# A macaron block on one core: the up projections' fast products as wide matmuls on high and low parts side by side

## The chip, the cores and the metric

The kernel runs on one core of a Trainium2 chip. The metric is the device time of one execution in microseconds. Five engines work beside each other, each on its own queue of instructions in a fixed order: TensorE (PE, with its weight loads shown apart as PEld) multiplies matrices into eight banks of accumulation memory (PSUM); VectorE (DVE) and ScalarE (ACT) work on elements; GpSimd (POOL) and SyncE (SP) here mostly issue DMA transfers.

## The reference

Input x has 512 tokens of 1024 features, all in float32. The block is a feed-forward network with half weight (ffn1), a mixer of a short convolution and chunked gated linear attention, a second feed-forward network (ffn2) and a last norm.

```python
def swiglu(x, w_gu, w_down):
    g, u = jnp.split(x @ w_gu, 2, axis=-1)
    return (jax.nn.silu(g) * u) @ w_down
...
x = x + 0.5 * swiglu(rmsnorm(x, norm_ffn1_g), ffn1_w_gu, ffn1_w_down)   # 1024 -> 2 x 2816 -> 1024
x = x + hybrid_mixer(rmsnorm(x, norm_mix_g), ...)
x = x + 0.5 * swiglu(rmsnorm(x, norm_ffn2_g), ffn2_w_gu, ffn2_w_down)
return rmsnorm(x, final_norm_g)
```

The change is in `x @ w_gu` of both feed-forward networks, the up products.

## The kernel before, in words

**Precision.** A float32 product is made of three: every factor is split into a rounded high part and the remainder, its low part, and the kernel sums weight-high × input-high, weight-high × input-low and weight-low × input-high. A weight tile is cast by ScalarE to its high part (`wh`, L331) and VectorE subtracts to get the low part (`wl`, L332). Three buffers of each exist.

**Fast products.** Most of an up product is done in *sets*. A set takes 256 columns of g and 256 of u, 512 tokens in two halves of 256, and 1024 features in two halves, and computes its 2 × 2 × 2 block product with seven products in place of eight, named m1, p2, q6, p5, q7, p4, p3. Each has 512 features, 256 columns and 256 tokens. There are nine sets in each feed-forward network; the first columns are plain products (L366 and L380). The weights' side of the seven products is built in memory from four loaded blocks a11, a12, a21, a22, each 512 KB (128 × 1024 floats): S3 = a11 + a21 by VectorE (L318); then, by DMAs that accumulate into their target (L309, issued by GpSimd), a21 += a22, a11 += a21 and a12 += a11. m1 reads a11 before its add and q6 reads it after; p2 reads a12 before its add and p3 after; q7 reads S3. Ten slots hold these tiles, and a load (L291, issued by SyncE) into a slot waits until its last reader is done. So a11's slot can take a new load only once a12's add has read it, and of the tiles that S3 sums one is loaded into such a slot. The tokens' side (`Operands`) is built once per feed-forward network, during its first set.

**One product** (`Set.run`, L479 on) is 24 matmuls (L502) of 128 columns of weights against 256 tokens: three kinds of high and low, four feature tiles, two halves of columns `e`. The two halves share one bank of 512 floats. Products accumulate into shared banks named a, b, c: m1, q6, q7 and p4 add up in b, p2 in a, p5 and p3 in c. What must be kept on the way is copied out by ScalarE (L507, L510). In every set but the first, m1 is copied from bank b into bank a (L507, the *fork*), and p2 adds onto it, so that bank a ends as g of one token half. Six banks circulate.

**Order.** The Python program writes the instructions down in the order in which each engine gets them, save that a scheduler lets an instruction pass another where their inputs allow. `order()` (L76) lists the products; `Weights.issue` runs three products ahead of the matmuls, so casts, low parts and DMAs of a product stand in the queues that far ahead. `done()` (L722 on) hangs the work on results behind a product: the silu of g (L727, L740), u (L730), and the products of the two (L734, L476). In the second feed-forward network `natural()` transposes one of eight tiles of x after a set's p3 (L771) by TensorE, and ScalarE copies it back (L772).

Of the kernel before, what the change touches and what calls it, by code (L numbers as in the profile page):

```python
# [8 lines left out]
F32 = mybir.dt.float32  # L9
F32R = mybir.dt.float32r  # L10
# [83 lines left out]

PLAIN1, PLAIN2 = 4, 4
PLAN = []
STEPS = []
# [6 lines left out]
        PLAN.append(u)  # L106


def sets(mat, pairs):
# [70 lines left out]
def block_kernel(ctx: ExitStack, tc: tile.TileContext, xT, vecs, gf, gup, wgl, wts, out):  # L180
# [6 lines left out]
    ps = ctx.enter_context(tc.tile_pool(name="ps", bufs=6, space=bass.MemoryType.PSUM))  # L187
    pa = ctx.enter_context(tc.tile_pool(name="pa", bufs=2, space=bass.MemoryType.PSUM))

    cnt = [0]  # L190
# [11 lines left out]
    def tile_of(pool, shape, dtype=F32):  # L202
        cnt[0] += 1
        return pools[pool].tile(shape, dtype, tag=pool, name=f"{pool}{cnt[0]}")

    def T(dtype=F32):
        return tile_of("tp", [P, S], dtype)

    def MM():
        cnt[0] += 1  # L210
        return ps.tile([P, S], F32, tag="mm", name=f"mm{cnt[0]}")

    def AUX():
        cnt[0] += 1
# [24 lines left out]
    class Weights:  # L239
# [239 lines left out]
    class Set:  # L479
# [34 lines left out]
        def first(self):  # L514
# [4 lines left out]
            nc.vector.tensor_tensor(out=t, in0=self.bank["a"], in1=self.v["m1"], op=ALU.add)  # L519
            return t  # L520

    class Operands:

        ORDER = ("m1", "p2", "p5", "q6", "q7", "p4", "p3")

        def __init__(self, b):
            self.b = b
            self.parts = {}  # L530
            self.sums = set()

# [19 lines left out]
        def make(self, p):  # L552
            if p in self.parts:
                return
            i = self.ORDER.index(p)
            if i > 0:
                self.make(self.ORDER[i - 1])
            v = self.sum(p)
            h, l = (tile_of("op", [P, 1024], F32R) for _ in range(2))
            hv, lv = (t.rearrange("p (k t) -> p k t", t=HW) for t in (h, l))  # L560
            nc.scalar.copy(hv, v)
            nc.vector.tensor_tensor(out=lv, in0=v, in1=hv.bitcast(F32), op=ALU.subtract)
            self.parts[p] = (h, l)
# [86 lines left out]
    def ffn(up, down, norm, nxt, plain, at):  # L650
        xh, xl = norm.h, norm.l
        rows = []

        def finish(k):
            if k == at:
# [64 lines left out]
        def up_set(i):  # L720
            h = new_hid()

            def done(s, p):
                bank, v = s.bank, s.v
                if p == "p2":
                    s.g1 = T()
                    nc.scalar.activation(s.g1, s.first(), AF.Silu)  # L727
                if p == "q7":
                    u2 = T()
                    nc.vector.scalar_tensor_tensor(out=u2, in0=bank["c"], scalar=-1.0, in1=v["q7"],  # L730
                                                   op0=ALU.mult, op1=ALU.subtract)
                    s.u2 = u2
                if p == "p4":
                    nc.vector.scalar_tensor_tensor(  # L734
                        out=h[:, :, :HW], in0=pair(bank["b"]), scalar=-1.0, in1=pair(s.g1),
                        op0=ALU.mult, op1=ALU.mult)
                if p == "p3":
                    g2 = T()
                    nc.vector.tensor_tensor(out=g2, in0=bank["c"], in1=v["q6"], op=ALU.add)
                    nc.scalar.activation(g2, g2, AF.Silu)  # L740
                    mul(h[:, :, HW:], pair(s.u2), pair(g2))
                    if nxt is None and i < KD:
                        natural(i)
                    for w in range(WIDE):
                        if i == 4 * w + 4 - plain // 2:
                            downs.append(down_operands(w))
                            downs[w].early()

            return Set(xo, done)

        def pair(t):
            return t.rearrange("p (e t) -> p e t", t=HW)

        run_sets(up_set)

        def split_hid(k):

# [4 lines left out]
            return h, l  # L762

        down_product(full(down, KF), split_hid, downs, nxt)

    def natural(i):

# [736 lines left out]
    with phase("small2", f=1, tp=6, v=4, qk=2, g=1, y=4, small=1):  # L1504
        W.phase(4, 5)
        n2 = Norm(V_G2)
        mixer(nm, n2)
# [46 lines left out]
```

## Time and profile before

| | |
|---|---|
| median of 3 runs | 1181.64 us (1181.12 to 1182.07) |
| the profiled execution | 1180.99 us |
| its span, first to last instruction | 1179.3 us |
| granted TensorE clock, mean | 0.999 of full |
| up sets of ffn1, from the chain | 50.15 to 231.58 us |
| up sets of ffn2, from the chain | 878.47 to 1063.37 us |
| matmuls of 256 columns in sets (L502), all stages | 3584 + 1792 |

An entry such as "L332 DVE TENSOR_TENSOR wl<-f,wh" means line 332 of the program, run on VectorE, writing a `wl` tile from an `f` and a `wh` tile. In the groups of instructions the columns are total busy time, mean duration in ns, and the idle time of the engine just before, with what ended it. In the chain of waits a row is start, length, engine and line. In the windows the columns are TensorE busy, its weight loads, VectorE, ScalarE, GpSimd, then granted clock, DMA share and GB/s. A waits row names who waited for whom, the total, how often, and the longest.

### The profile page before, as it was taken

The page shows a single profiled execution, that of the slowest core. Times are in us where ns is not written, and L with a number is a line of the kernel's source. Part 1 is how long each engine was busy: PE and PEld are TensorE (multiplying, and loading weights), DVE is VectorE, ACT ScalarE, POOL GpSimd, SP SyncE. Part 2 cuts the span into 40 slices and gives each one's busy share as a digit, 9 for nine tenths or more (in the row PEclk, how much of TensorE's full clock was granted, in tenths as well). Part 3 has the DMA queues.
Part 4 walks back from the last instruction along what each step waited for, and adds up shares of the span by engine and source line. Part 5 has one row for each costly group of instructions (what it writes and reads, how often), then busy time and mean ns, then how long its engine had stood idle before and what let it go on. Part 6 is the DMA issues. An engine that isn't in the chain of part 4 may idle for free.

```text
span 1179.3 us, 19168 instructions
## 1 busy us (share of the span) xinstructions
PE 1170.9 (99%) x7794; PEld 1080.7 (92%) x7794; DVE 868.9 (74%) x1027; ACT 634.3 (54%) x790; POOL 117.4 (10%) x153
## 2 busy tenths in 40 slices
PE   9999999999999999999999999999999999999997
PEld 8899999988888889999999998998889999998886
DVE  7985656896568965767697787685598566579955
ACT  6564455674435655565565576544355554566543
POOL 0010101101010111100110100000001111001100
PEclk9999999999999999999999999999999999999999
DMA  9388777678524388777677766531638767757721
GB/s 350 79 210 197 171 193 178 158 199 206 212 85 113 87 207 223 189 180 200 180 196 192 199 199 186 141 109 44 232 68 211 181 180 175 190 153 186 178 83 72
DMA packets 62600, 200.25 MB, mean 170 GB/s; under 512 B 6864, under 2 KB 13136, under 8 KB 62512
## 3 DMA queue, kind: packets, MB, share of 16 engines
q0 software_dynamic: 18784, 68.17, 31.7%
q1 hardware_dynamic: 39088, 126.37, 30.9%
q10 hardware_dynamic: 4640, 4.49, 1.1%
q8 instruction: 61, 1.00, 0.3%
q14 instruction: 27, 0.22, 0.1%
HBM read 124.55 MB, written 8.39 MB: 113 GB/s over the span
## 4 chain that ended last, share of the span: by engine, by line
PE 97%; ACT 1%; issue 1%; DVE 1%; ACTq 0%; POOL 0%; POOLq 0%
PE mm L502 53%; PE mm L625 12%; PE mm L366 11%; PE mm L380 7%; PE mm L838 4%; PE aux L625 4%; PE aux L838 1%; PE aux L1161 1%; PE aux L1142 1%; PE aux L1120 1%; PE aux L1164 0%; PE aux L224 0%; PE aux L1121 0%; PE mm L857 0%; PE aux L771 0%
## 5 line engine op out<-in xcount | busy, mean ns | idle before, releaser
L331 ACT CAST wh<-f 128x1024 fp32r<-128x1024 f32 (+1 forms) x341 | 356.2, 1047 | 406.3 <-PE mm L502 207.4
L332 DVE TENSOR_TENSOR wl<-f,wh 128x1024 fp32r<-128x1024 f32 (+1 forms) x341 | 413.3, 1217 | 154.1 <-ACT wh L331 141.3
L502 PE MATMUL mm<-op,wh 128*128 128x256 f32 x3584 | 471.1, 284 | 0.4 <-ACT mm L507 0.4
L502 PEld LDWEIGHTS mm<-op,wh 128*128 128x128 f32 x3584 | 447.9, 192 | 2.2 <-ACT mm L507 0.8
L502 PE MATMUL mm<-op,wl 128*128 128x256 f32 x1792 | 251.5, 283 | 0.0
L502 PEld LDWEIGHTS mm<-op,wl 128*128 128x128 f32 x1792 | 231.2, 192 | 0.1
L309 POOL DMA_DIRECT2D f<-f x126 | 108.9, 869 | 929.0 <-DVE wl L332 542.2
L625 PE MATMUL mm<-wh,op 128*128 128x512 f32 x432 | 106.9, 389 | 0.0
L625 PEld LDWEIGHTS mm<-wh,op 128*128 128x128 f32 x432 | 80.9, 188 | 16.7
L366 PE MATMUL mm<-op,wh 128*128 128x512 f32 x384 | 91.0, 389 | 0.0
L366 PEld LDWEIGHTS mm<-op,wh 128*128 128x128 f32 x384 | 72.0, 188 | 14.9
L380 PE MATMUL mm<-op,wh 128*128 128x512 f32 x256 | 64.2, 393 | 0.0
L625 PE MATMUL mm<-wl,op 128*128 128x512 f32 x216 | 57.7, 389 | 0.0
L380 PEld LDWEIGHTS mm<-op,wh 128*128 128x128 f32 x256 | 48.1, 189 | 10.3
L318 DVE TENSOR_TENSOR f<-f,f 128x1024 f32<-128x1024 f32 x42 | 51.3, 1222 | 0.8
L625 PEld LDWEIGHTS mm<-wl,op 128*128 128x128 f32 x216 | 40.6, 188 | 8.4
L366 PE MATMUL mm<-op,wl 128*128 128x512 f32 x192 | 47.4, 389 | 0.0
L366 PEld LDWEIGHTS mm<-op,wl 128*128 128x128 f32 x192 | 36.0, 188 | 7.5
L510 ACT COPY tp<-mm 128x512 f32<-128x512 f32 x68 | 39.6, 583 | 0.0
L601 DVE TENSOR_TENSOR op<-hidw,op 128x1024 fp32r<-128x1024 f32 x28 | 34.0, 1219 | 1.1 <-ACT op L600 1.0
L380 PE MATMUL mm<-op,wl 128*128 128x512 f32 x128 | 34.3, 389 | 0.0
L416 ACT ACTIVATE op<-X,vec 128x512 fp32r<-128x512 f32 x23 | 16.5, 719 | 31.8 <-DVE X L859 24.3
(269 smaller groups left out, 1042.5 us busy)
## 6 DMA issues: line engine op xcount, KB each, us to landing
f<-wts SPq DMA_DIRECT2D x219, 512.0 KB, 4.5
f<-f POOLq DMA_DIRECT2D x126, 512.0 KB, 5.3
X<-xT SPq DMA_DIRECT2D x8, 256.0 KB, 5.3
xs<-X POOLq DMA_DIRECT2D x8, 256.0 KB, 2.3
ga<-tp ACTq DMA_DIRECT2D x8, 256.0 KB, 3.2
gb<-tp ACTq DMA_DIRECT2D x8, 256.0 KB, 4.7
tp<-ga SPq DMA_DIRECT2D x8, 256.0 KB, 4.3
y<-tp SPq DMA_DIRECT2D x7, 256.0 KB, 2.3
```

Source lines behind the costliest of these rows:

```text
L309: return nc.gpsimd.dma_start(out_, a, accum_op=ALU.add).ins
L318: nc.vector.tensor_tensor(out=s3, in0=a11, in1=a21, op=ALU.add)
L331: self.cast = nc.scalar.copy(h[:, :w], raw[:, :w]).ins
L332: nc.vector.tensor_tensor(out=l[:, :w], in0=raw[:, :w], in1=h[:, :w].bitcast(F32), op=ALU.subtract)
L366: nc.tensor.matmul(o, w[:, i * P : (i + 1) * P], a[k], start=j == k == 0, stop=j == 2 and k == kt - 1)
L380: nc.tensor.matmul(o[c], w[:, s : s + P], a[k], start=k == 0 and j == 0, stop=k == kt - 1 and j == 2)
L416: nc.scalar.activation(xh[k], x[k], AF.Copy, scale=g)
L502: nc.tensor.matmul(to, ww[:, s], aa[:, t], start=fresh and k == 0 and e == 0 and j == 0, stop=k == 3 and j == 2, skip_group_check=True)
L510: nc.scalar.copy(v, o)
L601: nc.vector.tensor_tensor(out=lv, in0=v, in1=hv.bitcast(F32), op=ALU.subtract)
L625: nc.tensor.matmul(o[t], aa[:, s], ww[:, i * 512 : (i + 1) * 512], start=fresh and j == k == 0, stop=j == 2 and k == 3, skip_group_check=True)
L838: nc.tensor.matmul(o[t][e], b if j == 1 else a, wl if j == 2 else wh, start=k == K0 and e == 1 and j == 0, stop=k == KF - 1 and j == 2, sk ...
```

## The change

For the up sets of both feed-forward networks, three things change; the mixer and the down products keep the old class.

First, the tokens' operand of a product is stored with its high and low parts side by side for every feature tile (`Both`). Eight wide matmuls (weight-high against 512 columns: 256 high, 256 low) replace sixteen, and eight narrow ones (weight-low against the 256 high) stay. High and low sums now lie beside each other in a whole bank, and the two halves `e` take one bank each, so a product has a pair of banks (`PairSet`). The sum of the high and low columns is made when a result is read out: by two copies and an add (`taken`, for q6 and p5), by two adds onto a tile (`both`), or by a copy and an add (`whole`).

Second, there are three pairs of banks, x, y, z, handed on from set to set, opened for this stage only. The fork copies a whole pair, 1024 elements.

Third, the products' order: p3 comes before the next set's m1, and p4 after it (`up_order`). `natural()` and the early part of the down product's operands now hang behind p4.

```diff
+def up_order(firsts):
+    seq = []
+    for i, s in enumerate(firsts):
+        if i == 0:
+            seq += [(s, "m1"), (s, "p2")]
+        seq += [(s, "q6"), (s, "p5"), (s, "q7"), (s, "p3")]
+        if i + 1 < len(firsts):
+            t = firsts[i + 1]
+            seq += [(t, "m1"), (s, "p4"), (t, "p2")]
+        else:
+            seq += [(s, "p4")]
+    return seq
...
-    sets(up, [(s * HW, DFF + s * HW) for s in range(plain // 2, KF // 2)])
+    sets(up, [(s * HW, DFF + s * HW) for s in range(plain // 2, KF // 2)], up_order)
...
+    def banks():
+        cnt[0] += 1
+        stack = ExitStack()
+        pools["ps"] = stack.enter_context(tc.tile_pool(
+            name=f"ps{cnt[0]}", bufs=6, space=bass.MemoryType.PSUM, reuse_waits="tile"))
+        return stack
     def MM():
         cnt[0] += 1
-        return ps.tile([P, S], F32, tag="mm", name=f"mm{cnt[0]}")
+        return pools["ps"].tile([P, S], F32, tag="mm", name=f"mm{cnt[0]}")
+    def MM2(tag):
+        cnt[0] += 1
+        return pools["ps"].tile([P, 2, S], F32, tag=tag, name=f"{tag}_{cnt[0]}", bufs=1)
...
+    class Both:
+        def __init__(self, v):
+            self.t = []
+            for i in range(2):
+                t = tile_of("op", [P, 2, 2, HW], F32R)
+                w = v[:, 2 * i : 2 * i + 2]
+                nc.scalar.copy(t[:, :, 0], w)
+                nc.vector.tensor_tensor(out=t[:, :, 1], in0=w, in1=t[:, :, 0].bitcast(F32),
+                                        op=ALU.subtract)
+                self.t.append(t)
+        def high(self, k):
+            return self.t[k // 2][:, k % 2, 0]
+        def both(self, k):
+            return self.t[k // 2][:, k % 2].rearrange("p a t -> p (a t)")
+    def pair(t):
+        return t.rearrange("p (e t) -> p e t", t=HW)
+    class PairSet:
+        BANK = {"m1": "b", "p2": "a", "q6": "b", "p5": "c", "q7": "b", "p4": "b", "p3": "c"}
+        def __init__(self, group_, done, i):
+            self.group = group_
+            self.done = done
+            self.tags = {n: "xyz"[(i + j) % 3] for j, n in enumerate("bac")}
+            self.bank = {}
+        def left(self, n):
+            return self.bank[n][:, :, :HW]
+        def right(self, n):
+            return self.bank[n][:, :, HW:]
+        def open(self, n):
+            self.bank[n] = MM2(self.tags[n])
+            return self.bank[n]
+        def run(self, p):
+            n = self.BANK[p]
+            fresh = n not in self.bank
+            o = self.open(n) if fresh else self.bank[n]
+            x_ = self.group.get(p)
+            h, l = W.take()
+            for k in range(4):
+                for e in range(2):
+                    nc.tensor.matmul(o[:, e], h[:, k * HW + e * P : k * HW + (e + 1) * P],
+                                     x_.both(k), start=fresh and k == 0, stop=False,
+                                     skip_group_check=True)
+            for k in range(4):
+                for e in range(2):
+                    nc.tensor.matmul(o[:, e, :HW], l[:, k * HW + e * P : k * HW + (e + 1) * P],
+                                     x_.high(k), start=False, stop=k == 3,
+                                     skip_group_check=True)
+            if p == "m1" and self.forked:
+                nc.scalar.copy(self.open("a"), o)
+            elif p in ("m1", "q6", "p5"):
+                self.taken(p, n)
+            self.done(self, p)
+        def taken(self, p, n):
+            v, r = T(), T()
+            nc.scalar.copy(pair(v), self.left(n))
+            nc.scalar.copy(pair(r), self.right(n))
+            nc.vector.tensor_tensor(out=v, in0=v, in1=r, op=ALU.add)
+            setattr(self, p, v)
+        def both(self, n, t):
+            for part in (self.left(n), self.right(n)):
+                nc.vector.tensor_tensor(out=pair(t), in0=part, in1=pair(t), op=ALU.add)
+        def whole(self, n):
+            t = T()
+            nc.scalar.copy(pair(t), self.right(n))
+            nc.vector.tensor_tensor(out=pair(t), in0=self.left(n), in1=pair(t), op=ALU.add)
+            return t
...
+            if self.kind is not None:
+                self.parts[p] = self.kind(v)
+                return
...
-        xo = Operands(normed)
+        xo = Operands(normed, Both)
...
             def done(s, p):
-                bank, v = s.bank, s.v
                 if p == "p2":
-                    s.g1 = T()
-                    nc.scalar.activation(s.g1, s.first(), AF.Silu)
+                    if s.forked:
+                        s.g1 = s.whole("a")
+                    else:
+                        s.g1 = s.m1
+                        s.both("a", s.g1)
+                    nc.scalar.activation(s.g1, s.g1, AF.Silu)
                 if p == "q7":
-                    u2 = T()
-                    nc.vector.scalar_tensor_tensor(out=u2, in0=bank["c"], scalar=-1.0, in1=v["q7"],
-                                                   op0=ALU.mult, op1=ALU.subtract)
-                    s.u2 = u2
+                    s.both("b", s.p5)
                 if p == "p4":
+                    t = s.whole("b")
                     nc.vector.scalar_tensor_tensor(
-                        out=h[:, :, :HW], in0=pair(bank["b"]), scalar=-1.0, in1=pair(s.g1),
+                        out=h[:, :, :HW], in0=pair(t), scalar=-1.0, in1=pair(s.g1),
                         op0=ALU.mult, op1=ALU.mult)
                 if p == "p3":
-                    g2 = T()
-                    nc.vector.tensor_tensor(out=g2, in0=bank["c"], in1=v["q6"], op=ALU.add)
-                    nc.scalar.activation(g2, g2, AF.Silu)
-                    mul(h[:, :, HW:], pair(s.u2), pair(g2))
+                    s.both("c", s.q6)
+                    nc.scalar.activation(s.q6, s.q6, AF.Silu)
+                    nc.vector.scalar_tensor_tensor(
+                        out=h[:, :, HW:], in0=pair(s.p5), scalar=-1.0, in1=pair(s.q6),
+                        op0=ALU.mult, op1=ALU.mult)
+                if p == "p4":
                     if nxt is None and i < KD:
                         natural(i)
                     for w in range(WIDE):
@@ -746,12 +866,13 @@
                             downs.append(down_operands(w))
                             downs[w].early()
-            return Set(xo, done)
-        def pair(t):
-            return t.rearrange("p (e t) -> p e t", t=HW)
+            return PairSet(xo, done, i)
+        stage.close()
+        stage = banks()
         run_sets(up_set)
+        stage.close()
+        stage = banks()
         def split_hid(k):
@@ -762,6 +883,7 @@
             return h, l
```

How the rows move, at three places of which the prediction speaks. The names are `wh`, `wl` for parts of weights, `f` for a slot's tile, `tp` for a tile of 512 columns, x, y, z and `mm` for banks, `aux` for a bank of transposes.

**ScalarE, in the first set of ffn1, around the fork of the second set.** Before (`mm_754` is the fork's bank, `f_418` the second set's a11, read at `wh_791` after its add):

```order
L510 COPY tp_720<-mm_547 128x512
L561 CAST op_756<-hidw_356 128x1024
L331 CAST wh_760<-f_228 128x1024
L507 COPY mm_754<-mm_724 128x512
L331 CAST wh_791<-f_418 128x1024
L331 CAST wh_821<-f_416 128x1024
L727 ACTIVATE tp_819<-mm_754 128x512
```

After (`z_760` is the fork's pair, `f_468` the second set's a11; `wh_682` reads it before the add, for m1, and `wh_762` after it, for q6):

```order
L358 CAST wh_682<-f_468 128x1024
L358 CAST wh_714<-f_225 128x1024
L358 CAST wh_739<-f_473 128x1024
L358 CAST wh_762<-f_468 128x1024
L358 CAST wh_788<-f_466 128x1024
L857 ACTIVATE tp_638<-tp_638 128x512
L609 COPY z_760<-y_738 128x1024
```

The fork's copy stood ahead of the cast for q6; it stands behind the casts for q6 and p5 and a silu now.

**VectorE, between the second and third set of ffn1.** Before (`f_685` is the next set's a11, `f_919` the S3 of the set behind it):

```order
L332 TENSOR_TENSOR wl_885<-f_685,wh_884 128x1024
L332 TENSOR_TENSOR wl_923<-f_420,wh_922 128x1024
L318 TENSOR_TENSOR f_919<-f_915,f_913 128x1024
L332 TENSOR_TENSOR wl_956<-f_690,wh_955 128x1024
L730 SCALAR_TENSOR_TENSOR tp_952<-mm_883,tp_950 128x512
L332 TENSOR_TENSOR wl_987<-f_423,wh_986 128x1024
```

After (`f_888` is the next set's a11, `f_1073` the S3 of the set behind it):

```order
L359 TENSOR_TENSOR wl_1020<-f_712,wh_1019 128x1024
L345 TENSOR_TENSOR f_1073<-f_1069,f_1067 128x1024
L619 TENSOR_TENSOR tp_1013<-tp_1013,tp_1014 128x512
L359 TENSOR_TENSOR wl_1045<-f_888,wh_1044 128x1024
L619 TENSOR_TENSOR tp_1039<-tp_1039,tp_1040 128x512
L625 TENSOR_TENSOR tp_1039<-z_919,tp_1039 128x512
L359 TENSOR_TENSOR wl_1077<-f_709,wh_1076 128x1024
L625 TENSOR_TENSOR tp_1039<-z_919,tp_1039 128x512
L625 TENSOR_TENSOR tp_1013<-y_1018,tp_1013 128x512
```

S3's add stood two rows behind m1's low part; it stands two rows ahead of it now, and operations on results stand between the low parts.

**TensorE, where the sets of ffn2 begin.** After:

```order
L393 MATMUL mm_8371<-op_8012,wl_8288 128x512 x2
L893 MATMUL aux_8653<-ident,X_7531 128x128 x4
L893 MATMUL aux_8840<-ident,X_7531 128x128 x4
L893 MATMUL aux_9027<-ident,X_7531 128x128 x4
L893 MATMUL aux_9215<-ident,X_7531 128x128 x2
L600 MATMUL x_8426<-op_8228,wh_8342 128x512 x4
```

Before, the last plain matmul (L366) was followed at once by m1 (L502), and the first transposes (L771) stood at the end of the first set; 14 of the 32 stand ahead of the first set's m1 now.

More of the change, by code (lines that the diff above doesn't have):

```diff
@@ L106, in units, with sets @@
         PLAN.append(u)
-def sets(mat, pairs):
+def sets(mat, pairs, order=order):
     firsts = []
@@ L186, in block_kernel @@
     keep = ctx.enter_context(tc.tile_pool(name="keep", bufs=1))
-    ps = ctx.enter_context(tc.tile_pool(name="ps", bufs=6, space=bass.MemoryType.PSUM))
     pa = ctx.enter_context(tc.tile_pool(name="pa", bufs=2, space=bass.MemoryType.PSUM))
@@ L522, in block_kernel, with __init__ @@
     class Operands:
         ORDER = ("m1", "p2", "p5", "q6", "q7", "p4", "p3")
-        def __init__(self, b):
+        def __init__(self, b, kind=None):
             self.b = b
+            self.kind = kind
             self.parts = {}
@@ L747, in done @@
                             downs[w].early()
-            return Set(xo, done)
-        def pair(t):
-            return t.rearrange("p (e t) -> p e t", t=HW)
+            return PairSet(xo, done, i)
+        stage.close()
+        stage = banks()
         run_sets(up_set)
+        stage.close()
+        stage = banks()
         def split_hid(k):
@@ L764, in ffn @@
         down_product(full(down, KF), split_hid, downs, nxt)
+        stage.close()
     def natural(i):
@@ L1506, in block_kernel @@
         n2 = Norm(V_G2)
-        mixer(nm, n2)
+        with banks():
+            mixer(nm, n2)
     with phase("small3", **FFN):
```

## The prediction, on record before the result

> **What bounds the kernel now.** I read the page's busy times and chain first, then the chain in order of time, then the two up stages by windows, then their groups, and last single engines where the change moves rows.
>
> ```profile
> PE 1170.9 (99%) x7794; PEld 1080.7 (92%) x7794; DVE 868.9 (74%) x1027; ACT 634.3 (54%) x790; POOL 117.4 (10%) x153
> PE 97%; ACT 1%; issue 1%; DVE 1%; ACTq 0%; POOL 0%; POOLq 0%
> 28.39 21.76 PE mm L366 x96
> 50.15 181.43 PE mm L502 x1512
> 904.39 0.44 PE aux L771 x4
> 904.82 20.16 PE mm L502 x168
> 50.15:231.58 181.43, 181.43 (x1513) 181.43 (x1513) 127.28 (x126) 98.87 (x118) 24.00 (x28) 1.00 0.74 181
> 878.47:1063.37 184.90, 184.90 (x1546) 184.90 (x1545) 126.68 (x126) 102.65 (x126) 24.16 (x28) 1.00 0.73 179
> ```
>
> TensorE bounds it. In the whole up stage of the first ffn the chain is one unbroken piece of 1512 matmuls, at full clock; in the second ffn it breaks only for transposes (0.44 us of four). The two windows are these stages: TensorE busy to the last hundredth, VectorE 127.28/181.43 = 70%, ScalarE 54%, DMA 74%. So a TensorE saving counts in full only while the work behind it keeps up, and a wait that does not exist now counts in full.
>
> **TensorE's saving.** L502: 181.43/1512 = 120.0 ns for 256 columns. L366, the plain products of 512 columns: 21.76/96 = 226.7 ns. So 256 columns more cost 106.7, and each matmul has 13.3 ns beside its columns. A product was 24 × 120.0 = 2.880 us; it becomes 8 × 226.7 + 8 × 120.0 = 2.773. The columns are the same 6144; eight fixed parts go. With 2 × 9 × 7 = 126 products: 126 × 0.1067 = **−13.44 us**. A set goes from 20.16 to 19.42 us.
>
> The Trainium skill (TensorE: Matmul & The Clock Gate, section "Back-to-back issue gap") gives an isolated warm gap of N/2.4 + 2.5 ns. By it the saving would be 126 × 8 × 2.5 ns = 2.5 us, an estimate from that page; the rows above give 13.3 ns where it has 2.5, and decide.
>
> **What is added beside it.** Both halves of the tokens now lie in two banks that must be summed.
>
> ```profile
> L332 DVE TENSOR_TENSOR wl<-f,wh 128x1024 fp32r<-128x1024 f32 x63 | 76.8, 1222 | 32.8 <-ACT wh L331 31.1 <-DMA f<-wts 1.6
> L318 DVE TENSOR_TENSOR f<-f,f 128x1024 f32<-128x1024 f32 x10 | 12.2, 1223 | 0.2
> L739 DVE TENSOR_TENSOR tp<-mm,tp 128x512 f32<-128x512 f32 x8 | 5.5, 692 | 10.4 <-PE mm L502 10.4
> 57.51 0.68 DVE L519 TENSOR_TENSOR tp<-mm,tp 128x512 f32<-128x512 f32 x1
> 58.11 1.22 DVE L546 TENSOR_TENSOR hidw<-hidw 128x1024 f32<-128x1024 f32 x1
> 59.24 2.35 DVE L332 TENSOR_TENSOR wl<-f,wh 128x1024 fp32r<-128x1024 f32 x2
> 51.54 1.05 ACT L331 CAST wh<-f 128x1024 fp32r<-128x1024 f32 x1 [6.56 <-DMA f<-f]
> 52.50 0.62 ACT L697 ACTIVATE tp<-tp 128x512 f32<-128x512 f32 x1
> 53.03 1.03 ACT L561 CAST op<-hidw 128x1024 fp32r<-128x1024 f32 x1
> 53.97 1.05 ACT L331 CAST wh<-f 128x1024 fp32r<-128x1024 f32 x1
> 54.91 0.57 ACT L510 COPY tp<-mm 128x512 f32<-128x512 f32 x1
> 55.39 1.05 ACT L331 CAST wh<-f 128x1024 fp32r<-128x1024 f32 x1
> ```
>
> From start to start, VectorE takes 0.60 us for 512 elements and 1.13 for 1024; ScalarE 0.95 for a 1024 cast, 0.53 for a silu, 0.48 for a copy of 512. Per set VectorE had seven low parts, one S3 and four small operations: 8 × 1.22 + 4 × 0.69 = 12.5 us of 20.16; now ten small ones: 16.7 of 19.42 (86%). ScalarE's copies of 512 go from two and a fork of 512 to six and a fork of 1024: +4 × 0.48 + 0.47 = 2.4 us, 13.4 of 19.42 (69%). On throughput both fit, so I cost their work at nothing inside a set, except where an order makes TensorE wait. The reads by VectorE of a pair of banks (two at once, 512 elements) have no row; I take L739's 0.69, bounds 0.69 and 1.22. I laid the changed order out by hand with these durations, each instruction starting when its engine is free and its inputs are there. Waits on TensorE appear in four places.
>
> **1. First set of the first ffn.** No earlier set covers it. q7's operands come behind q6's copies on ScalarE and two sums on VectorE: q7 1.6 to 2.0 us late, others 0.8 together. The large one is the second set's p2. It adds onto the copy of m1 (the fork), and that copy has moved on ScalarE from ahead of the q6 cast to behind it, another cast and a silu. The q6 cast reads a11 after an accumulating DMA. What such DMAs take:
>
> ```profile
> f<-f POOLq DMA_DIRECT2D x126, 512.0 KB, 5.3
> L309 POOL DMA_DIRECT2D f<-f x1: 856/856/856, 121.0 to 121.0; - x1
> DMA to landing us min/median/max: 4.5/4.5/4.5
> ...
> L309 POOL DMA_DIRECT2D f<-f x1: 856/856/856, 125.1 to 125.1; - x1
> DMA to landing us min/median/max: 4.9/4.9/4.9
> ...
> L309 POOL DMA_DIRECT2D f<-f x1: 856/856/856, 126.7 to 126.7; - x1
> DMA to landing us min/median/max: 6.5/6.5/6.5
> ...
> L291 SPq DMA_DIRECT2D f<-wts x1: 327/327/327, 129.3 to 129.3; - x1
> DMA to landing us min/median/max: 5.2/5.2/5.2
> ACT wh L331 <- DMA f<-f: 8.0, 2, 6.6
> ACT wh L331 <- PE mm L502: 63.1, 48, 2.2
> ```
>
> Alone 4.5; the second of an overlapping pair 6.5; the casts already wait for one at the stage's start (6.6). In my layout the DMA is issued 5.1 us before p2 is due, so at a landing of 5.1 p2 waits 0.95 + 0.95 + 0.53 + 1.05 = 3.5 us, at 5.9 4.3 us. Sum of the set: 1.9 + 0.8 + 3.5 = **+6.2**, bounds 5.7 and 8.
>
> **2. First set of the second ffn.** 14 of the 32 transposes now stand ahead of m1; their 14 × 0.11 = 1.5 us is only moved. But the third group reuses a bank that ScalarE must copy out, and that copy is queued behind a cast that waits for an accumulating DMA: 0.4 to 1.8 us, then 1.3 to 2.4 for p2 as above. **+3.0**, bounds 2.0 and 4.2.
>
> **3. The ends.** The last p4 directly follows p3, and adds into the bank that VectorE must first read twice for u (0.60, a low part of 1.13, 0.69, and a sum of 1.13 ahead): 0.7 to 2.0 us late. The down product then starts in p4's second bank, free only after a silu, a copy and an add (0.53 + 0.48 + 0.69 and what is queued there): 2.0. **+3.3 per ffn**, 6.6, bounds 5.4 and 8.
>
> **4. The loop through the weights, in every middle set.** S3's add moves on VectorE ahead of m1's low part, and it waits for two loads. So a loop closes: a11 lands → a12's add lands (4.5 alone, 5.3 the median) → load, issued 0.33 later for its pair, lands (5.2) → S3's add 1.13, a small add 0.60, m1's low part 1.22 → a11's add, the second of a pair, lands (6.5). With 4.5: 4.5 + 0.33 + 5.2 + 2.95 + 6.5 = 19.5; with 5.3: 20.3; with a load of 4.5 and an add of 4.5: 18.8. A set lasts 19.42. What is over that stalls TensorE, each set anew: −0.6 (nothing) to +0.9. Some seven sets per ffn have such a loop, 14 in all. I take 0.3 a set: **+4.2**; bounds 0 and 14 × 0.9 = 12.6.
>
> Sum: −13.4 + 6.2 + 3.0 + 6.6 + 4.2 = +6.6 us. On the profiled run's 1180.99 that is 1187.6; it stood 0.65 below the median of 1181.64, so against that median **1188**. With all low bounds: −13.4 + 5.7 + 2.0 + 5.4 + 0 = −0.3; with all high: −13.4 + 8 + 4.2 + 8 + 12.6 = +19.4.
>
> **What hides what.** The work behind q6's copies, the sums of p3 and q7 and the second casts is hidden by TensorE's other products of a set (5.5 us between the end of q7 and the end of m1). If that cover is gone, a set costs VectorE's own 16.7 plus its waits, still not over 19.42. The mixer and the down products keep their order on every engine, so they get no term.
>
> **Rivals.**
>
> *The saving is kept.* The stage edges cost less than laid out because the queues run ahead (ScalarE was idle over 40% of the stage), and the loop stays at 18.8. For it: TensorE waits nowhere today, and the casts stand idle 63.1 us of the stage for TensorE alone (the last row quoted); against: the fork's place in the queue is in the order itself, whatever the durations. With half of the edge terms (7.9) and no loop: 1181.6 − 13.4 + 7.9 = 1176. Chance 0.14.
>
> *Waits cancel the saving.* The edges as laid out, no loop: 1181.6 − 13.4 + 15.8 = 1184, or by the low bounds 1181. Half of this lies within 0.2% (2.4 us, about what a measurement can tell from no change). Chance 0.28.
>
> *The loop decides.* If the adds, now bunched behind each other with the loads at 74% DMA share, take 0.8 us more each (two in the loop) than in my sum, each set is 1.6 + 0.3 = 1.9 us late: 14 × 1.9 = 26.6 in place of 4.2, 1210; with half of that lateness 1199. It decides from a loop of 20 us. For it: 6.5 is the present second-of-a-pair, and the pair will be closer; against: a stalled TensorE also slows the demand for DMA. Chance 0.2.
>
> *The change doesn't save what it says.* The 13.3 ns go with each matmul only if they belong to the matmul. If four fifths of them belong to its columns after all, the saving is 2.7 us and the sum comes to 1188 + 10.7 = 1199. The rows of L502 and L366 speak against it: their difference is what 256 columns cost, whatever the fixed part is. Chance 0.05. The Trainium skill's gap, quoted above, is of this kind: 2.5 ns of fixed part.
>
> **How the numbers follow.** The forecast (edges and a small loop, 1185 to 1192) has 0.33; the rest is as given. Faster by over 0.2%: the first rival 0.14 and a little of the second, 0.16. Same: most of the second, 0.23. Slower: the forecast, the third, the last and a part of the second, 0.61. The range: leaving out about 0.1 on each side gives 1176 to 1203; the forecast's own is 1185 to 1192.
>
> **What would show it.** In the changed kernel: matmuls of 226.7 and 120.0 ns in the sets, so that TensorE's busy time in the two stages falls by 13.4; TensorE waiting on ScalarE's fork copy, once per set, longest in each ffn's first set (3 to 4.5 us); a wait of 2 us where the first down matmuls begin; ScalarE's q6 cast waiting for an accumulating DMA in every set, and VectorE's S3 for loads. If no fork wait stands in the middle sets, term 4 is wrong; if TensorE's matmuls differ from 226.7, the saving is; if VectorE rather than a DMA ends the waits in the middle sets, its 86% is the bound, not the loop.

## The result, and where the time went

The change makes the kernel slower: 1224.68 us in the median (1220.48 to 1227.94) against 1181.64, a ratio of 1.0362 (95% interval 1.0345 to 1.0380). The prediction had the sign, but said 1188, with a range up to 1203.

The changed kernel's page:

```profile
span 1224.7 us, 17422 instructions
PE 1176.6 (96%) x6786; PEld 1035.2 (85%) x6786; DVE 934.0 (76%) x1151; ACT 675.4 (55%) x876; POOL 117.3 (10%) x153
```

Its stages (the windows are: up to the first set, the sets of ffn1, down to the end of the mixer and ffn2's plain products, the sets of ffn2, the rest; columns as before):

```profile
0.00:50.60 50.60, 48.57 (x214) 39.93 (x214) 43.40 (x71) 28.84 (x41) 3.22 (x11) 1.00 0.66 229
50.60:251.00 200.40, 183.27 (x1007) 159.01 (x1008) 156.71 (x182) 116.14 (x155) 24.79 (x29) 0.97 0.69 167
251.00:904.10 653.10, 647.17 (x4046) 583.04 (x4045) 485.51 (x599) 351.62 (x443) 57.44 (x77) 1.00 0.61 163
904.10:1108.30 204.20, 188.33 (x1044) 163.57 (x1042) 159.56 (x186) 122.24 (x166) 24.98 (x29) 0.97 0.69 169
1108.30:1224.70 116.40, 109.31 (x479) 89.67 (x479) 88.81 (x118) 56.54 (x73) 6.89 (x8) 0.99 0.44 118
```

The span grew by 45.4 us. The sets of ffn1 took 200.4 in place of 181.4 (+19.0), those of ffn2 204.2 in place of 184.9 (+19.3). Between them are +6.2 (653.1 against 878.47 − 231.58 = 646.9), of which 1.9 are a wait at the start of the down product; the first and the last stage have 0.9 together. VectorE did 65 us more work, and is at 78% in the sets: busy, not full.

TensorE's waits in the sets of ffn1 and at their end, those over 0.3 us, in order of time (start, length, and in brackets the idle time before, with what ended it):

```profile
50.85 2.08 PE L600 MATMUL x<-op,wh 128*128 128x512 f32 x8 [0.54 <-DVE tp L503]
63.59 2.08 PE L600 MATMUL x<-op,wh 128*128 128x512 f32 x8 [1.34 <-DVE op L558]
79.02 3.57 PE L600 MATMUL z<-op,wh 128*128 128x512 f32 x8 [3.60 <-ACT z L609]
101.46 2.11 PE L600 MATMUL x<-op,wh 128*128 128x512 f32 x8 [1.05 <-ACT x L609]
122.96 2.11 PE L600 MATMUL y<-op,wh 128*128 128x512 f32 x8 [1.68 <-ACT y L609]
145.93 2.12 PE L600 MATMUL z<-op,wh 128*128 128x512 f32 x8 [3.15 <-ACT z L609]
168.42 3.49 PE L600 MATMUL x<-op,wh 128*128 128x512 f32 x8 [2.67 <-ACT x L609]
210.52 2.12 PE L600 MATMUL z<-op,wh 128*128 128x512 f32 x8 [1.30 <-ACT z L609]
232.07 3.13 PE L600 MATMUL x<-op,wh 128*128 128x512 f32 x8 [1.73 <-ACT x L609]
248.22 2.11 PE L600 MATMUL z<-op,wh 128*128 128x512 f32 x8 [0.37 <-DVE tp L625]
253.37 1.88 PE L741 MATMUL mm<-wh,op 128*128 128x512 f32 x7 [1.86 <-DVE tp L631]
```

The first three rows are the first set, the last two the end: 5.5 and 2.2 us, about what was laid out. The rows between are the forked p2 of the middle sets (one of them, near 189, waits for nothing and has no row), and there the sum went wrong: from 79.02 to 232.07 are seven sets in 153.05 us, 21.9 each, where TensorE's own work is 19.55 (below).

Follow one round of the loop. The rows are the transfers, with their time of issue: an a11 add (112.6), the a12 add behind it (120.8), the second of the three loads that follow at 125.5, 125.9 and 127.6, and the next a11 add (136.2):

```profile
L336 POOL DMA_DIRECT2D f<-f x1: 860/860/860, 112.6 to 112.6; - x1
DMA to landing us min/median/max: 7.7/7.7/7.7
...
L336 POOL DMA_DIRECT2D f<-f x1: 862/862/862, 120.8 to 120.8; - x1
DMA to landing us min/median/max: 4.5/4.5/4.5
...
L318 SPq DMA_DIRECT2D f<-wts x1: 1394/1394/1394, 125.9 to 125.9; - x1
DMA to landing us min/median/max: 6.9/6.9/6.9
...
L336 POOL DMA_DIRECT2D f<-f x1: 860/860/860, 136.2 to 136.2; - x1
DMA to landing us min/median/max: 7.1/7.1/7.1
```

And VectorE and ScalarE at the places of the loop, in order of time:

```profile
132.93 1.23 DVE L345 TENSOR_TENSOR f<-f,f 128x1024 f32<-128x1024 f32 x1 [2.72 <-DMA f<-wts]
134.68 1.22 DVE L359 TENSOR_TENSOR wl<-f,wh 128x1024 fp32r<-128x1024 f32 x1
...
143.39 1.04 ACT L358 CAST wh<-f 128x1024 fp32r<-128x1024 f32 x1 [6.05 <-DMA f<-f]
144.34 0.63 ACT L857 ACTIVATE tp<-tp 128x512 f32<-128x512 f32 x1
144.87 1.00 ACT L609 COPY z<-y 128x1024 f32<-128x1024 f32 x1
```

a11 lands at 120.3; GpSimd issues a12's add 0.5 later, which takes 4.5; the second load is issued at 125.9 and takes 6.9; S3's add starts at 132.93, m1's low part ends at 135.9, the next a11 add is issued at 136.2 and takes 7.1, and a11 lands at 143.3. That is 23.0 us from landing to landing. Behind it ScalarE's cast, silu and fork copy follow without a gap, and p2 starts at 145.93.

This is one of the longer rounds. There are 13 of them, seven in ffn1 and six in ffn2, and read in the same way they take 21.0 to 23.8 us, 22.2 in the mean. The load of 6.9 belongs to this round: in the round before, three loads were issued as close together (104.1, 104.6 and 106.1) and the second took 4.7; in the round behind, the second took 4.8.

```profile
L318 SPq DMA_DIRECT2D f<-wts x1: 504/504/504, 104.6 to 104.6; - x1
DMA to landing us min/median/max: 4.7/4.7/4.7
```

One set of ffn2 has no such round. There S3's add stands behind m1's low part in the changed kernel too:

```profile
1006.98 1.22 DVE L359 TENSOR_TENSOR wl<-f,wh 128x1024 fp32r<-128x1024 f32 x1 [0.63 <-ACT wh L358]
...
1008.72 1.22 DVE L345 TENSOR_TENSOR f<-f,f 128x1024 f32<-128x1024 f32 x1
```

a11's add is issued at 1008.5, ahead of S3's; a11 lands 18.6 us after the landing before it, and p2 (at 1017.78) does not wait.

### The profile page after: what moved, and what is told of

Same layout as the page of the kernel before. It is cut to its first block, busy times and chain, and to the rows that moved or that the text cites. A ratio compares the mean times of both kernels' runs of the same rounds, so it can differ in the third digit from the quotient of the medians.

```text
span 1224.7 us, 17422 instructions
## 1 busy us (share of the span) xinstructions
PE 1176.6 (96%) x6786; PEld 1035.2 (85%) x6786; DVE 934.0 (76%) x1151; ACT 675.4 (55%) x876; POOL 117.3 (10%) x153
## 5 line engine op out<-in xcount | busy, mean ns | idle before, releaser
L529 PE MATMUL mm<-op,wh 128*128 128x256 f32 x1568 | 208.1, 284 | 2.2 <-ACT tp L537 1.8
L529 PEld LDWEIGHTS mm<-op,wh 128*128 128x128 f32 x1568 | 196.9, 191 | 4.1 <-ACT tp L537 2.3
L529 PE MATMUL mm<-op,wl 128*128 128x256 f32 x784 | 110.0, 283 | 0.0
L600 PE MATMUL z<-op,wh 128*128 128x512 f32 x336 | 90.4, 414 | 18.1 <-ACT z L609 15.9
L529 PEld LDWEIGHTS mm<-op,wl 128*128 128x128 f32 x784 | 101.2, 192 | 0.1
L600 PE MATMUL x<-op,wh 128*128 128x512 f32 x336 | 87.5, 403 | 8.4 <-ACT x L609 6.5
L600 PEld LDWEIGHTS z<-op,wh 128*128 128x128 f32 x336 | 63.7, 199 | 31.9 <-ACT z L609 17.1
L600 PE MATMUL y<-op,wh 128*128 128x512 f32 x336 | 85.1, 395 | 5.4 <-ACT y L609 5.3
L393 PEld LDWEIGHTS mm<-op,wh 128*128 128x128 f32 x384 | 72.0, 188 | 14.9
L600 PEld LDWEIGHTS x<-op,wh 128*128 128x128 f32 x336 | 61.9, 194 | 21.3 <-ACT x L609 7.3
L600 PEld LDWEIGHTS y<-op,wh 128*128 128x128 f32 x336 | 60.7, 190 | 17.1 <-ACT y L609 6.0
L407 PE MATMUL mm<-op,wh 128*128 128x512 f32 x256 | 64.2, 392 | 1.2 <-DVE op L440 0.6
L407 PEld LDWEIGHTS mm<-op,wh 128*128 128x128 f32 x256 | 47.6, 188 | 12.1 <-DVE X L1603 1.0
```

Of the source, the lines that this page charges most:

```text
L393: nc.tensor.matmul(o, w[:, i * P : (i + 1) * P], a[k], start=j == k == 0, stop=j == 2 and k == kt - 1)
L407: nc.tensor.matmul(o[c], w[:, s : s + P], a[k], start=k == 0 and j == 0, stop=k == kt - 1 and j == 2)
L529: nc.tensor.matmul(to, ww[:, s], aa[:, t], start=fresh and k == 0 and e == 0 and j == 0, stop=k == 3 and j == 2, skip_group_check=True)
L600: nc.tensor.matmul(o[:, e], h[:, k * HW + e * P : k * HW + (e + 1) * P], x_.both(k), start=fresh and k == 0, stop=False, skip_group_check= ...
```

## The experiments

Two causes can look like this. In theory L the closed loop (each round of it needs the landing of the round before) sets the length of a set. In theory F each set is late by a fixed amount, because the fork's copy stands behind a cast that waits for a DMA. Theory V says that VectorE is too full, and theory C that the slow clock after each wait is what costs.

**S3's add behind m1's low part.** Only VectorE's order is changed:

```diff
-                nc.vector.tensor_tensor(out=s3, in0=a11, in1=a21, op=ALU.add)
+                with tc.issue_after(self.low) if self.low is not None else ExitStack():
+                    nc.vector.tensor_tensor(out=s3, in0=a11, in1=a21, op=ALU.add)
...
             if p == "m1":
+                self.low = low    # the low part just written
```

> The changed kernel with one thing moved: on VectorE, S3's add of the next set but one stands behind m1's low part again, as before the change (it stood ahead of it); ScalarE's order, the wide matmuls and all else stay. Theory L (the loop): the middle sets of the changed kernel are late because a closed loop of a11's add, a12's add, loads, S3's add, m1's low part and a11's add takes 22 to 23 us against a set of 19.4. With S3's add behind m1's low part the loop is open: the waits for the fork in the middle sets (21.7 us in all) go, and with them about half of the slow-clock stretches, 1195 us (1190 to 1200); the first set's wait of 3.6 us stays. Theory F (the fork's place in ScalarE's queue is the cause, a fixed lateness in each set): no gain beyond 5 us, 1220 or more. Theory V (VectorE is too full with the added sums): no gain, 1222 to 1228.

1195.69 us (1.0119, interval 1.0104 to 1.0134): 29 us of the 43 are gone. Every wait of TensorE in the sets and at their ends, ffn1:

```profile
50.82 2.08 PE L604 MATMUL x<-op,wh 128*128 128x512 f32 x8 [0.53 <-DVE tp L507]
63.56 2.08 PE L604 MATMUL x<-op,wh 128*128 128x512 f32 x8 [1.34 <-DVE op L562]
78.99 3.78 PE L604 MATMUL z<-op,wh 128*128 128x512 f32 x8 [3.58 <-ACT z L613]
233.53 2.11 PE L604 MATMUL z<-op,wh 128*128 128x512 f32 x8 [0.77 <-DVE tp L629]
238.67 1.89 PE L745 MATMUL mm<-wh,op 128*128 128x512 f32 x7 [1.86 <-DVE tp L635]
```

Between 79 and 233 us nothing is left, though the fork stands where it stood, VectorE does the same work and the products are the same. F and V fall for the middle sets. a11's add is no shorter with the loop open:

```profile
L338 POOL DMA_DIRECT2D f<-f x1: 862/862/862, 132.9 to 132.9; - x1
DMA to landing us min/median/max: 7.3/7.3/7.3
```

**The fork ahead of q6's cast.** The edit moves a cast of ScalarE. In the trace VectorE's order changes with it in some places (the product of two results in L860 comes ahead of q6's low part), but S3's add and m1's low part keep their order:

```diff
-            self.cast = nc.scalar.copy(h[:, :w], raw[:, :w]).ins
+            with tc.issue_after(self.fork) if p == "q6" and self.fork is not None else ExitStack():
+                self.cast = nc.scalar.copy(h[:, :w], raw[:, :w]).ins
```

> The changed kernel with one thing moved: on ScalarE, the cast for q6 (which waits for a11's accumulating DMA) is queued behind the fork's copy and not ahead of it; VectorE's order stays. Theory L: the loop goes on, the wait only moves from p2 to q6 in each middle set, with about 4 us won once per feed-forward network: 1210 to 1218. Theory F: p2 waits no more and q6 has 2.8 us more slack than the lateness of most sets: the 21.7 us of the middle sets, 6 us of the first sets and most of the slow clock go, 1183 to 1192. Theory V: the wait only changes its name, 1220 to 1228.

1221.28 us (1.0329, 1.0307 to 1.0351): 3 us better. L expected 1210 to 1218, F 1183 to 1192, V 1220 to 1228. The size is V's, which the first run had ruled out, and L's range was missed too; what decides is the length of a set. Three p2 that follow the fork in neighbouring sets, and S3's add ahead of the second:

```profile
138.92 2.12 PE L602 MATMUL z<-op,wh 128*128 128x512 f32 x8 [0.79 <-ACT z L611]
...
151.03 1.23 DVE L346 TENSOR_TENSOR f<-f,f 128x1024 f32<-128x1024 f32 x1 [2.35 <-DMA f<-wts]
...
160.49 2.11 PE L602 MATMUL x<-op,wh 128*128 128x512 f32 x8 [0.80 <-ACT x L611]
...
182.29 2.12 PE L602 MATMUL y<-op,wh 128*128 128x512 f32 x8 [0.79 <-ACT y L611]
```

The sets are still 21.6 and 21.8 us long. These two are among the longer ones: from 95.87 to 224.33 six sets take 21.4 each. TensorE's waits are spread over several products of a set now, 0.3 to 0.9 us each; VectorE still waits for a load ahead of S3's add, and the loop's pace is about the same. L's 4 us per feed-forward network were 3 in all.

**Both moves.**

> Both moves together: S3's add behind m1's low part, and the fork ahead of q6's cast. Theory L: no loop and no fork wait, what stays is the saving of 13.4 us, the waits for operands in the first sets and at the ends (some 7 us) and what the mixer lost (4 us): 1175 to 1186. Theory F: as with the fork alone, 1183 to 1192. Theory V: over 1215.

1187.27 us (1.0046, 1.0031 to 1.0061), a little above L's 1175 to 1186. With the loop open the fork's place counts, 8 us; with it closed it counted 3. Here TensorE runs a middle set without a wait, and the price of a product can be read:

```profile
115.74 2.00 PE L605 MATMUL y<-op,wh 128*128 128x512 f32 x8
117.58 1.11 PE L610 MATMUL y<-op,wl 128*128 128x256 f32 x8
118.53 2.00 PE L605 MATMUL x<-op,wh 128*128 128x512 f32 x8
```

From start to start the eight wide matmuls take 1.84 us (230 ns each), the narrow ones 0.95 (119 ns): 2.79 us a product, 19.55 a set. The saving is 126 × (2.880 − 2.793) = 11.0 us, where 13.4 were expected from L366's 226.7 ns.

**The order of products alone,** with the old class and its narrow matmuls:

```diff
-    sets(up, [(s * HW, DFF + s * HW) for s in range(plain // 2, KF // 2)])
+    sets(up, [(s * HW, DFF + s * HW) for s in range(plain // 2, KF // 2)], up_order)
...
                     mul(h[:, :, HW:], pair(s.u2), pair(g2))
+                if p == "p4":
                     if nxt is None and i < KD:
                         natural(i)
```

> The kernel before with the new order of products alone (p3 ahead of the next m1, p4 behind it; the work that hung behind p3 for the end of a set now behind p4), with the old class, its single banks and its 24 narrow matmuls. In the order of instructions S3's add stands ahead of m1's low part, and q6's cast ahead of the fork, as in the changed kernel; VectorE's work is that of before. Theory L: a loop of 21 to 22 us against a set of 20.16: 1 to 2 us late in each of 14 sets and some slow clock, 1200 to 1215. Theory F: the same sign, some 2 us a set, 1200 to 1215. Theory V: VectorE has no more work than before, 1180 to 1186.

1215.53 us (1.0293, 1.0275 to 1.0310), at the upper end of what L and F expected alike (1200 to 1215) and far from V's 1180 to 1186. So most of the loss is in the order, with VectorE at its old load. The first and the last forked p2 of ffn1's middle sets, four others between them:

```profile
98.56 2.18 PE L518 MATMUL mm<-op,wh 128*128 128x256 f32 x16 [1.44 <-ACT mm L523]
...
207.69 2.18 PE L518 MATMUL mm<-op,wh 128*128 128x256 f32 x16 [1.72 <-ACT mm L523]
```

109.13 us for five sets, 21.8 each. With TensorE's work at 19.55 a set it was 21.9 (the changed kernel) and 21.4 (the fork moved), and at 20.16 it is 21.8: the length is the loop's, and these differences in TensorE's work do not show in it.

**A link taken out:** the changed kernel without a12 += a11 in these sets. This leaves work out: p3 then multiplies a12 alone.

```diff
-            if p == "p2":
+            if p == "p2" and n not in IN_UP:    # IN_UP: the sets of w_gu
                 self.add(a12, a11)
```

> The changed kernel without the accumulating DMA a12 += a11 in the sets of the feed-forward networks (18 DMAs less, so p3 multiplies a12 without a11: work left out); the order on VectorE and ScalarE is the same row by row. Theory L: a12's add is a link of the loop, since the next loads wait for its landing. Without it the first load waits only for q6's low part and the second for p5's, some 0.6 to 2.9 us earlier, and the loads have one DMA less beside them (6.9 us to landing should come to 5 to 6): the loop falls from 23 to 20 to 21.5 us, 0.5 to 2 us a set still over 19.5: 1197 to 1212. If the loads wait for something else, no change, 1220 to 1228.

1207.57 us (1.0224, 1.0195 to 1.0253), within L's range, with the rows of VectorE and ScalarE in the same order. From the forked p2 at 101.02 to that at 226.73:

```profile
101.02 2.11 PE L603 MATMUL x<-op,wh 128*128 128x512 f32 x8 [1.05 <-ACT x L612]
...
226.73 2.14 PE L603 MATMUL x<-op,wh 128*128 128x512 f32 x8 [2.34 <-ACT x L612]
```

six sets in 125.71 us, 21.0 each; the sets differ, and at the end of three of the six TensorE waits 0.4 us or less for the fork. The loop is shorter by about 1 us, not by the 5 us of a12's add, since the second load still waits for p5's low part (in one round that ends at 123.42, and the load is issued at 123.44). The run also moves fewer bytes, so it can't say how much of it is the link and how much the lighter DMA.

**The clock.** After some waits the first matmuls of the changed kernel took 3.57 or 3.49 us for eight in place of 2.1, and its windows show why (here 80 to 85 us; the last column but two is the clock):

```profile
80.00:85.00 5.00, 5.00 (x22) 4.19 (x21) 3.18 (x5) 1.63 (x2) 0.12 (x1) 0.73 0.90 187
```

Both up stages had 0.97, and the whole execution 0.989. To see whether that costs, 16 small matmuls without use stand ahead of each forked p2:

```diff
+            if p == "p2" and self.forked:
+                f_ = AUX()
+                with tc.issue_after(W.last):
+                    for _ in range(16):
+                        g_ = nc.tensor.matmul(f_[:, :P], ones_r, ones_r, start=True, stop=True).ins
```

> The changed kernel with 16 small matmuls of 128 columns (about 1.7 us, without use for the result) ahead of the forked p2 of every set but the first, where TensorE waits for the fork's copy. They keep TensorE busy through most of a wait, so that its clock should not fall behind one. Theory L (the loop, which TensorE has no part in, sets a set's length, and the slow matmuls after a wait only fill what would be waited anyway): 1218 to 1230, as without them. Theory C (the slow clock after waits costs its excess of busy time, 8 to 9 us per feed-forward network): 1205 to 1212.

1227.96 us (1.0393, 1.0377 to 1.0409). The profiled execution:

```profile
core 0: 1224.2 us, clock 0.997
```

In the profiled execution the clock is back, but for a stretch in each network's first sets, and the time is not; the other three executions had 0.992 to 0.994, against 0.989 to 0.992 of the changed kernel's four. Most of the slow matmuls lie inside the round of the loop, and the runs show no cost of them there. Theory C, 1205 to 1212, falls.

**VectorE's room,** with the loop open as in the first run, and S3's add done twice in each set:

```diff
                     nc.vector.tensor_tensor(out=s3, in0=a11, in1=a21, op=ALU.add)
+                    if n in IN_UP:
+                        nc.vector.tensor_tensor(out=s3, in0=a11, in1=a21, op=ALU.add)
```

> S3's add behind m1's low part as in the run e1_sum_later, and S3's add done twice in every set of the feed-forward networks: VectorE gets 1.2 us more per set, 17.9 of 19.42, with the loop open. Theory L: VectorE still has room, within 3 us of that run's 1195.7. Theory V in a weak form (VectorE's load decides once the loop is open): 18 sets by up to 1.1 us more, 1205 to 1215.

1197.32 us (1.0133, 1.0118 to 1.0148), 1.6 above the run without the double add, with intervals that overlap. Eighteen adds of 1.2 us would be 21: VectorE has room for them.

**Old class, new order, both moves.**

> The old class with its narrow matmuls, the new order of products, and both moves (S3's add behind m1's low part, the fork ahead of q6's cast). It says what the order costs once the loop is open, and, against the run with both moves and the wide matmuls (1187.3), what the wide matmuls bring. Theory L: 1182 to 1186 (the old time and a few us at the edges), so that the wide matmuls with all that hangs on them bring nothing or lose 1 to 5 us, their 13.4 us being used up at the edges and in the mixer. If the order costs more than the loop and the fork's place, 1190 to 1200.

1189.51 us (1.0069, 1.0052 to 1.0086), above the 1182 to 1186 expected. The order costs some 8 us even with the loop open. TensorE's longer waits in its trace lie at the edges of the two stages and make 3.1 us; the rest isn't assigned. Against the same with wide matmuls (1.0046) the wide ones, with all that hangs on them, gain about 2, which the intervals don't tell from nothing.

**The edges.** At the start of the down products TensorE waits for the last operations on p4's result, 2.6 and 1.9 us with both moves; my reading was that the product needs a bank of p4's pair. A first try gave the first product other tiles:

```diff
-        A = [MM(), MM()]
+        M = [MM() for _ in range(6)]
+        A = [M[0], M[3]]
...
+            banks = {"a": A, "b": [AUX(), AUX()] if w else [M[2], M[5]],
+                     "c": [MM(), MM()] if w else [M[1], M[4]]}
```

> Both moves, and the first down product in the pair of banks that the last set's p2 has left (it took one bank of p4's pair). The waits of 2.6 and 1.9 us at the start of the down products, and the slow clock behind the second, should go: 1187.3 less 4.5 to 6.5, so 1180 to 1184. If those waits only turn into a wait of the next product, 1186 to 1188.

1187.48 us (1.0050, 1.0035 to 1.0065), and the same wait stood there, 2.6 and 1.9 us. My reading is that banks are given out in the order in which tiles are first used, so that the product had one bank of p4's pair again; the trace does not name banks, so this is not shown, and the run tells nothing on the cause. The second try takes the two banks of the transposes:

```diff
-            banks = {"a": A, "b": [(MM, AUX)[w % 2]() for _ in range(2)], "c": [MM(), MM()]}
+            banks = {"a": A, "b": [(AUX, MM)[w % 2]() for _ in range(2)], "c": [MM(), MM()]}
```

> Both moves (1187.3), and the first down product in the two banks that the transposes use, the second wide group in the common ones. In the run e6 the first product had been given bank 7 of p4's pair again, so it tells nothing on this; now the product's banks are free. Theory: the waits of 2.6 and 1.9 us at the start of the down products and the slow clock behind the second go: 1180 to 1184. If the wait is for operands of that product and not for the bank: 1186 to 1188.5.

1179.78 us: 0.9986 of the kernel before (0.9977 to 0.9996), and TensorE runs on into the down product, so the wait was for the bank:

```profile
228.90 1.12 PE L610 MATMUL z<-op,wl 128*128 128x256 f32 x8
229.86 1.78 PE L746 MATMUL aux<-wh,op 128*128 128x512 f32 x7
```

Last, the token operands made three products ahead (`run_sets(up_set, ahead=3)`):

> As the run e12_down_aux, and the token operands of a set made three products ahead of their use (two before). The wait of 1.3 us for q7's operand in ffn1's first set should go and the 0.8 us of the fork may: 1 to 2 us less than that run, 1178 to 1183. If the earlier operands delay the copies of the first results on ScalarE as much, no change.

1179.06 us, 0.9984 (0.9975 to 0.9993), the best version: a small gain over the kernel before, whose interval excludes 1. Against the run before it nothing can be told apart. The wait of 1.3 us for q7's operand went, and waits of 0.75 us (shown) and 0.4 us took its place:

```profile
65.91 2.11 PE L605 MATMUL z<-op,wh 128*128 128x512 f32 x8 [0.75 <-ACT tp L623]
```

Where the saving goes can be read from the run before: TensorE is busy 1162.6 us in its profile against 1170.9 in the kernel before, and idle 15.7 against 8.4. The work is saved, and waits that were not there before use up nearly all of it.

## Why the prediction was wrong

**TensorE's saving:** right in kind, 11.0 us in place of 13.4. The term took 226.7 ns for a wide matmul from the plain products; in the sets it is 230. The sign laid down for it, TensorE's busy time in the two stages falling by 13.4, did not come: it rose, 183.3 and 188.3 against 181.4 and 184.9, with matmuls at a lower clock behind the waits. The rival by which the change saves only 2.7 us is out at 230 and 119 ns. The Trainium skill's gap (TensorE: Matmul & The Clock Gate, "Back-to-back issue gap"), from which 2.5 us followed as an estimate, comes to 216 and 109 ns for these two widths; the trace does not agree.

**The edges (terms 1 to 3):** near. First set of ffn1: 6.2 expected, 5.5 measured, the fork's 3.5 as 3.6. First set of ffn2: 3.0 expected, 2.7 measured. The ends: 3.3 each expected, 2.2 and 3.0 measured. That the mixer would get no term was wrong by some 4 us. Two new waits of TensorE there are named:

```profile
PE mm L529 <- ACT tp L537: 1.8, 2, 1.6
PE aux L1135 <- DVE g L1117: 1.3, 1, 1.3
```

The premise, that every engine keeps its order there, was wrong for the second: the gate product that waits (L1135, at 370.47) follows the high matmuls of L407 now; before, it followed the low ones and a product with the identity. For the first no change of order was found, and its cause stays open. The two runs with the old class and the new order have neither wait, so they come with the wide products or their banks. The last versions still have 1.2 to 1.6 us of the first and 0.5 of the second.

**The loop (term 4):** this is the step that failed. The loop was found, its links and its order were right, and the rival "the loop decides" described the outcome, but I gave it 0.2 and the forecast "0.3 a set". The sum of 19.5 us a round measured 22.2 in the mean of 13 rounds, and the sets of the middle lasted 21.9 in place of 19.55, some 32 us for 14 sets in place of 4.2:

| link | expected | the round shown | mean of 13 (range) |
|---|---|---|---|
| a11 landed to a12's add issued | 0 | 0.5 | 0.7 (0.5 to 1.8) |
| a12's add | 4.5 | 4.5 | 4.5 (4.5 to 4.7) |
| to the second load's issue | 0.33 | 0.6 | 0.6 (0.5 to 0.9) |
| the load | 5.2 | 6.9 | 5.1 (4.4 to 6.9) |
| load landed to the issue of a11's add | 2.95 | 3.4 | 3.7 (3.1 to 5.8) |
| a11's add | 6.5 | 7.1 | 7.6 (6.4 to 9.4) |

The load was priced rightly in the mean; only single rounds have a long one. Of the 2.7 us that are missing, a11's add has 1.1: 6.5 was its duration in the kernel before. It is 7.3 in the first run too, where the loop is open, so the loop does not account for it; what makes it longer is not shown. The other 1.7 are the times between a link's end and the next issue, left out as nothing. They include up to 2.5 us in which S3's add, its load landed, stood behind other rows of VectorE. Being a loop, it lost the whole excess again in each set; an error of 2.7 us in a chain that is passed once would have cost 2.7.

With these sizes the terms make some 39 us (−11.0 + 13.4 at the edges + 32.2 + 4.3 in the mixer) of the 45 by which the span grew; the rest isn't assigned.

**The mean of the cases:** the range gave 0.1 to all above 1203, though 1 us more in a round moves the result by some 14 us. The bounds of the links were durations of the kernel before, and none had been seen in the order that the change makes. The rival's arithmetic also slipped: half of its 26.6 us in place of 4.2 gives 1197, not 1199.

**The slow clock** was not in the prediction. It was real (0.97 in both stages), but inside the rounds it cost nothing that the runs could show. Behind the last fork of ffn1 eight wide matmuls took 3.13 us in place of 2.1; that lies outside the loop and may cost its 1 us.

## What to carry to other kernels

When a change reorders products, follow each queue for a loop: does an instruction that waits for a transfer now stand ahead of one that starts the chain to that same transfer a round later? Such a loop sets a pace of its own, whatever the busy engine saves. The short times between its links belong to the sum, and each set pays an error again. The test is cheap: if kernels with different work per round have the same round, the loop decides, and moving one row opens it.

## What the runs showed of the hardware that was not expected

- TensorE's clock fell for a few microseconds after some waits (0.73 in the window of 80 to 85 us), but not after all of them, and the length of the wait alone does not tell which: after 3.60, 2.67 and 1.73 us it did (eight wide matmuls in 3.57, 3.49 and 3.13 us), after 3.15 it did not (2.12).
- The wide matmuls cost 230 ns in the sets and 226.7 in the plain products, at one width and full clock.
- The issue of a load took SyncE 1.39 us once in ffn1 (the row at 125.9), where 0.33 is the rule and the same place in the neighbouring rounds has 0.50 and 0.34. That load landed after 6.9 us. The cause stays open.
